# Output stages of a macaron block: low halves of weights on VectorE, sums of activations stored and loaded

## The chip, the cores and the metric

One core of one Trainium2 chip runs the whole program. Time is device time in microseconds of one execution, and the figure for a kernel is the median of its runs. The engines named below are TensorE (PE: matrix products; PEld is its loading of the stationary operand), VectorE (DVE), ScalarE (ACT), GpSimd (POOL) and SyncE (SP, which issues nearly all DMAs here). Each has a queue of its own that is worked off in order.

## The reference

A decoder block on 1024 tokens of width 1024, all float32. The two SwiGLU layers are what this change is about.

```python
def swiglu(x, w_in, w_out):
    gate, up = jnp.split(x @ w_in, 2, axis=-1)      # w_in: 1024 x 5632
    return (jax.nn.silu(gate) * up) @ w_out         # w_out: 2816 x 1024

x = layer_norm(ALPHA * x + 0.5 * swiglu(x, ffn1_w_in, ffn1_w_out), ln1_g, ln1_b)
x = layer_norm(ALPHA * x + token_mixer(x, ...), ln2_g, ln2_b)
x = layer_norm(ALPHA * x + 0.5 * swiglu(x, ffn2_w_in, ffn2_w_out), ln3_g, ln3_b)
e = (p @ ple_w_in) * jax.nn.sigmoid(x @ ple_w_gate)
x = layer_norm(ALPHA * x + e, ln4_g, ln4_b)
```

## The kernel before

Every large float32 product is made of three passes over operands in a rounded format: `split` (lines 176 to 179) casts an operand to its high half on ScalarE and subtracts that from it, on VectorE unless another engine is given, to get the low half; high times high, high times low and low times high are summed in PSUM. Products of 2 x 2 blocks of matrices use Winograd's form of Strassen's scheme: seven block products instead of eight, with sums and differences of blocks on both sides.

**Input stage of a layer** (`ffn`, from line 473; `Pair`, from line 29). The 22 column blocks f of w_in are worked off in the order 0, 10, 1, 11, ..., 9, 19, 20, 21. For each, the weights come as four 256 KB tiles Ws, GpSimd combines them, and seven products of 12 matmuls run (L201). The result silu(gate)*up of 128 features by 1024 tokens lies in two halves g1 and g2 (tiles a) of 512 tokens. `store` writes them to DRAM tensors h, arranged by chunk c of the output stage. The blocks f and f + 10 are the two feature halves of one Strassen block: after f + 10, GpSimd makes from the kept halves of f (`kept`) and the new g2 the sum s2 = kept[1] + g2 - kept[0] in two instructions (lines 529 and 530), and s2 is stored in the place of kept[1]. Tags with few buffers set what may run ahead: T has 6, H and O have 4 each, Ws has 7 and A8 has 14.

**Output stage** (`out_chunk`, from line 576). There are 5 chunks c; chunk c covers the blocks 2c, 2c+1 and their partners. For each chunk `combine` (lines 560 to 574) loads four 128x512 tiles of w_out for each of two blocks j, makes the four combinations t1, t2, t3, t4 on GpSimd (L565, L567, L570, L572; t1, t2 and t4 one after the other in the same tile t), and `put` splits all seven into the tiles w11, wt1, ... (tag A8, so two chunks' worth exist). The low halves of these 14 are made on VectorE in chunk 0 and on GpSimd in chunks 1 to 4 (`gps if c else vec`, line 586). Then for each of the two halves sp of the tokens, ha and hb are loaded (512 KB each, line 594) and hold a11, s2, a12, a22; VectorE makes s1 = s2 + a11, s4 = a12 - s2 and s3 = a22 - s2 (lines 622, 626, 629, tiles s with tag T); each of seven activations is split to Wh and Wl and multiplied with its w (12 matmuls, L603), and VectorE adds the PSUM results into acc or into the sums u (L610, L620, L633). That is 168 matmuls a chunk. After the chunks the two blocks without a partner run in `out_phase` (L232), with the layer norm behind.

The kernel has two such layers, so two input and two output stages. The order of each engine's instructions is fixed when the program is built, by a list scheduler that goes by program order and by estimated times of instructions, so work of the next chunk is placed between that of the current one.

Of the kernel before, what the change touches and what calls it, by code (L numbers as in the profile page):

```python
# [8 lines left out]
F32 = mybir.dt.float32  # L9
# [3 lines left out]
ALU = mybir.AluOpType  # L13
P = 128
# [6 lines left out]
NPAIR = 10  # L21
# [87 lines left out]
class Block:  # L109
# [363 lines left out]
    def ffn(self, xs, w_in, w_out, acc, after, between, points, begun=(None, None), ahead=None, at=None, early=None):  # L473
        staged, later = begun
        nc = self.nc
        gps, vec = nc.gpsimd, nc.vector

        order = FIRST + list(range(2 * NPAIR, NFF))

        def pair(f):  # L480
            def begin(p):
                nc.scalar.activation(p.a1, p.b1, AF.Silu)
            return Pair(self, xs, lambda kh, up: w_in[f + NFF * up][kh], begin,
                        {(kh, up): t for (n, kh), t in (staged or {}).items() for up in range(2) if n == f + NFF * up})

        def products(p):

            marks = iter(range(points if not p.early else 0))

            def tick(ins):  # L490
                if next(marks, None) is not None:
                    with self.tc.issue_after(ins.ins):
                        next(between, None)

            p.rest(tick)
            nc.scalar.activation(p.a2, p.a2, AF.Silu)
            vec.tensor_tensor(p.a1, p.a1, p.c1, ALU.mult)
            tick(vec.tensor_tensor(p.a2, p.a2, p.c2, ALU.mult))
            return p.a1, p.a2

        pairs = self.in_pairs([lambda f=f: pair(f) for f in order], later)

        scale = 0.5 / ALPHA
        chunks = NPAIR // 2
        hd = {}
        for c in range(chunks):
            for kh in range(2):
                hd[c, kh] = self.dram.tile([2, P, 2, 2, 256], F32, tag=f"h{c}_{kh}", name=f"h{c}_{kh}")
        for f in range(2 * NPAIR, NFF):
            hd[f] = self.dram.tile([P, D], F32, tag=f"h{f}", name=f"h{f}")  # L510
        def store(f, th, g):
            if f < 2 * NPAIR:
                c, j = f % NPAIR // 2, f % 2
                dst = hd[c, f // NPAIR][:, :, th, j].rearrange("s p n -> p s n")
                nc.sync.dma_start(dst, g.rearrange("p (s n) -> p s n", n=256))
            else:
                nc.sync.dma_start(hd[f][:, th * 512:(th + 1) * 512], g)

        kept = None
        for i, (f, p) in enumerate(zip(order, pairs)):  # L520
            g1, g2 = products(p)
            store(f, 0, g1)
            if f < NPAIR:
                kept = g1, g2
            else:
                store(f, 1, g2)
            if NPAIR <= f < 2 * NPAIR:

                gps.tensor_tensor(kept[1], kept[1], g2, ALU.add)
                gps.tensor_tensor(kept[1], kept[1], kept[0], ALU.subtract)  # L530
                store(f - NPAIR, 1, kept[1])
            if i == at:
                for _ in between:
                    pass
                early()

        for _ in between:
            pass
        sums = [self.t("E", [P, 512], name="sum") for _ in range(4)]
        for c in range(chunks):  # L540
            self.out_chunk(c, w_out, hd, acc, sums, scale)

        for s in (0, 1, 2, 3, 4, 5, 6, 7):
            for dh in range(2):
                if s >= 4 or dh:
                    sl = slice(dh * 512, (dh + 1) * 512)
                    gps.tensor_tensor(acc[s][:, sl], acc[s][:, sl], sums[s % 4], ALU.add)
        if ahead is not None:
            ahead()
        hs, ws = [], []  # L550
        for f in range(2 * NPAIR, NFF):
            w = self.t("A8", [P, 2, D], F32R, name="wo")
            self.load_row(w_out[f * P:(f + 1) * P, :], w[:, 0], w[:, 1])
            h = [self.t("O", [P, D], F32R, name="hp") for _ in range(2)]
            self.load_row(hd[f], *h)
            hs.append(h)
            ws.append((w[:, 0], w[:, 1]))
        self.out_phase(hs, ws, acc, scale, self.pm, after=after)
# [17 lines left out]
    def out_chunk(self, c, w_out, hd, acc, sums, scale):  # L576


        nc = self.nc
        gps, vec = nc.gpsimd, nc.vector  # L580
        halves = [slice(0, 512), slice(512, 1024)]
        w = {n: self.t("A8", [P, 2, 2, 512], F32R, name="w" + n)
             for n in ("11", "t1", "21", "t2", "22", "t3", "t4")}
        for j in range(2):
            def put(n, y):
                self.split(y, w[n][:, j, 0], w[n][:, j, 1], gps if c else vec)

            b11, b12, b21, b22 = (self.stage(w_out[f * P:(f + 1) * P, halves[dh]])
                                  for f in (2 * c + j, NPAIR + 2 * c + j) for dh in range(2))
            self.combine(b11, b12, b21, b22, put)  # L590
        for sp in range(2):
            ha, hb = self.t("O", [P, 2, 512], name="ha"), self.t("H", [P, 2, 512], name="hb")
            for t, kh in ((ha, 0), (hb, 1)):
                nc.sync.dma_start(t, hd[c, kh][sp].rearrange("p t j n -> p t (j n)"))
            a11, s2, a12, a22 = ha[:, 0], ha[:, 1], hb[:, 0], hb[:, 1]

            def prod(ps, a, n, start=True):
                hh = self.split_w(a)
                for i in range(2):
                    for j in range(2):  # L600
                        cols = slice(256 * j + P * i, 256 * j + P * i + P)
                        for k, (p, q) in enumerate(((0, 0), (0, 1), (1, 0))):
                            nc.tensor.matmul(ps[i], hh[p][:, cols], w[n][:, j, q],  # L603
                                             start=(start and j == 0 and k == 0), stop=(j == 1 and k == 2),
                                             skip_group_check=not start)

            def add(ps, th, dh):
                for i in range(2):
                    t = acc[4 * th + 2 * sp + i][:, halves[dh]]
                    vec.scalar_tensor_tensor(t, ps[i], scale, t, ALU.mult, ALU.add)  # L610

            two = lambda: [self.pm(), self.pm()]
            u = sums[2 * sp:2 * sp + 2]
            b1 = two()
            prod(b1, a11, "11")
            for i in range(2):
                if c == 0:
                    nc.scalar.mul(u[i], b1[i], scale)
                else:
                    vec.scalar_tensor_tensor(u[i], b1[i], scale, u[i], ALU.mult, ALU.add)  # L620
            s1, s3, s4 = (self.t("T", [P, 512], name="s") for _ in range(3))
            vec.tensor_tensor(s1, s2, a11, ALU.add)
            b3 = two()
            prod(b3, s1, "t1")
            add(b3, 1, 1)
            vec.tensor_tensor(s4, a12, s2, ALU.subtract)
            prod(b1, a12, "21", start=False)
            add(b1, 0, 0)
            vec.tensor_tensor(s3, a22, s2, ALU.subtract)
            b2 = two()  # L630
            prod(b2, s2, "t2")
            for i in range(2):
                vec.scalar_tensor_tensor(u[i], b2[i], scale, u[i], ALU.mult, ALU.add)  # L633
            prod(b3, s4, "22", start=False)
            add(b3, 0, 1)
            b4 = two()
            prod(b4, s3, "t3")
            add(b4, 1, 1)
            prod(b4, a22, "t4", start=False)
            add(b4, 1, 0)  # L640
# [689 lines left out]
```

## Time and profile before

| | us |
|---|---|
| median of 3 runs | 2142.65 (2140.26 to 2145.51) |
| profiled execution | 2143.06 |
| its span, first to last instruction | 2141.3 |

| engine | busy us | share of the span |
|---|---|---|
| TensorE | 2008.5 | 94% |
| VectorE | 1682.1 | 79% |
| GpSimd | 1133.6 | 53% |
| ScalarE | 835.8 | 39% |

The page covers the whole program. The first output stage runs from about 474 to 700 us, the second from about 1754 to 1985 us; the input stages lie right ahead of them. Busy times by stretch say more than shares of the whole, since each stage has its own limit. One matmul of 128x512 is listed with some 0.39 us, but matmuls overlap: what counts is the distance from one start to the next. The same holds in part for VectorE, whose instructions overlap by a little.

### The profile page before, as it was taken

To read this page: it belongs to the slowest core of one execution; us is meant where nothing else is said; L and a number is where in the kernel's file an instruction comes from. 1 tells how busy PE (TensorE), PEld (TensorE's weight loads), DVE (VectorE), ACT (ScalarE), POOL (GpSimd) and SP (SyncE) were. 2 spreads that over 40 slices of the span, in tenths; PEclk is the share of its full clock that TensorE was granted. 3 is DMA by queue.
4 is the path that set the end of the run, shared out by engine and by line. 5 is a ranking of instruction groups with operands and counts; after the bars stand their busy time and mean duration, and the time that the engine had idled before them with its cause. 6 is when DMAs were issued, how large, how long until landed. Compare 5 with 4: busy or idle time off the path is not lost.

```text
span 2141.3 us, 26291 instructions
## 1 busy us (share of the span) xinstructions
PE 2008.5 (94%) x8982; PEld 1626.4 (76%) x8982; DVE 1682.1 (79%) x2514; ACT 835.8 (39%) x1492; POOL 1133.6 (53%) x754
## 2 busy tenths in 40 slices
PE   7998999998989899999998899999999998899988
PEld 5886778776768777888885677788888876678866
DVE  8789767678898976667668979966666688898998
ACT  5333333444342454343545524533333343333420
POOL 4646555458972364343236683564444458972360
PEclk9999999999999999999999999999999999999999
DMA  5323233543321254343472240242222243322111
GB/s 171 113 84 94 83 99 113 184 158 123 113 89 44 104 182 140 102 122 110 138 263 66 91 141 15 71 127 89 79 89 79 79 166 115 111 81 79 40 54 69
DMA packets 127702, 228.78 MB, mean 107 GB/s; under 512 B 14160, under 2 KB 43856, under 8 KB 127568
## 3 DMA queue, kind: packets, MB, share of 16 engines
q1 hardware_dynamic: 127568, 227.10, 33.0%
q8 instruction: 71, 1.16, 0.2%
q14 instruction: 63, 0.52, 0.1%
HBM read 174.12 MB, written 52.92 MB: 106 GB/s over the span
## 4 chain that ended last, share of the span: by engine, by line
PE 57%; DVE 20%; POOL 12%; issue 7%; DMA 3%; ACT 2%; SPq 0%; DVEq 0%; POOLq 0%; ACTq 0%
PE pm L201 42%; PE pm L603 7%; DVE Wl L179 3%; POOL wt L179 3%; PE pm L1251 2%; PE pm L212 2%; POOL w L179 2%; POOL t L567 1%; DVE acc L237 1%; PE pm L232 1%; POOL t L572 1%; DVE ln L251 1%; POOL Ws L570 1%; DVE ln L257 1%; POOL t L565 1%
## 5 line engine op out<-in xcount | busy, mean ns | idle before, releaser
L179 DVE TENSOR_TENSOR Wl<-Ws,Wh 128x512 fp32r<-128x512 f32 (+1 forms) x284 | 238.0, 842 | 138.9 <-ACT Wh L178 134.5
L178 ACT CAST Wh<-s 128x512 fp32r<-128x512 f32 (+1 forms) x264 | 158.8, 601 | 383.3 <-PE pm L201 136.1
L178 ACT CAST Wh<-Ws 128x512 fp32r<-128x512 f32 (+1 forms) x284 | 169.5, 597 | 339.3 <-PE pm L201 294.1
L179 DVE TENSOR_TENSOR Wl<-s,Wh 128x512 fp32r<-128x512 f32 (+1 forms) x264 | 227.2, 861 | 35.3 <-ACT Wh L178 35.1
L87 POOL TENSOR_TENSOR s<-s,Ws 128x512 f32<-128x512 f32 (+1 forms) x68 | 95.0, 1397 | 212.8 <-DVE Wl L179 208.0
L603 PE MATMUL pm<-wt,Wh 128*128 128x512 f32 x640 | 190.7, 395 | 2.9 <-ACT Wh L178 2.0
L105 POOL TENSOR_TENSOR u<-u,p 128x512 f32<-128x512 f32 x68 | 109.3, 1607 | 154.1 <-DVE u L95 126.6
L603 PE MATMUL pm<-w,Wh 128*128 128x512 f32 x480 | 149.4, 403 | 22.1 <-ACT Wh L178 17.7
L82 POOL TENSOR_TENSOR s<-Ws 128x512 f32<-128x512 f32 (+1 forms) x68 | 90.6, 1332 | 138.8 <-DVE Wl L179 97.8
L99 POOL TENSOR_TENSOR s<-Ws,s 128x512 f32<-128x512 f32 (+1 forms) x68 | 102.9, 1514 | 110.3 <-DVE Wl L179 110.3
L603 PEld LDWEIGHTS pm<-wt,Wh 128*128 128x128 f32 x640 | 121.5, 191 | 31.3 <-ACT Wh L178 4.8
L610 DVE SCALAR_TENSOR_TENSOR acc<-pm,acc 128x512 f32<-128x512 f32 x200 | 131.7, 681 | 15.6 <-PE pm L603 14.8
L603 PEld LDWEIGHTS pm<-w,Wh 128*128 128x128 f32 x480 | 91.4, 193 | 45.8 <-ACT Wh L178 21.8
L603 PE MATMUL pm<-wt,Wl 128*128 128x512 f32 x320 | 116.6, 398 | 5.5 <-DVE Wl L179 5.5
L603 PE MATMUL pm<-w,Wl 128*128 128x512 f32 x240 | 91.8, 407 | 15.4 <-DVE Wl L179 15.4
L201 PE MATMUL pm<-x11h,Wh 128*128 128x512 f32 (+1 forms) x264 | 99.6, 385 | 5.3 <-ACT x11h L178 4.8
L201 PE MATMUL pm<-x11h,Wl 128*128 128x512 f32 (+1 forms) x264 | 99.7, 380 | 3.3 <-DVE Wl L179 3.3
L201 PE MATMUL pm<-xt2h,Wl 128*128 128x512 f32 x240 | 95.3, 397 | 6.7 <-DVE Wl L179 6.7
L201 PE MATMUL pm<-x11l,Wh 128*128 128x512 f32 (+1 forms) x264 | 99.5, 380 | 2.0 <-DVE x11l L179 1.4
L201 PE MATMUL pm<-xt1h,Wl 128*128 128x512 f32 x240 | 95.0, 396 | 5.4 <-DVE Wl L179 5.3
L91 POOL TENSOR_TENSOR Ws<-Ws 128x512 f32<-128x512 f32 (+1 forms) x68 | 97.4, 1432 | 4.5
L201 PE MATMUL pm<-x21h,Wl 128*128 128x512 f32 x240 | 94.8, 396 | 5.0 <-DVE Wl L179 5.0
(384 smaller groups left out, 5867.1 us busy)
## 6 DMA issues: line engine op xcount, KB each, us to landing
Ws<-in_ffn_w_in SPq DMA_DIRECT2D x196, 256.0 KB, 2.7
Ws<-in_ffn_w_out SPq DMA_DIRECT2D x88, 256.0 KB, 2.9
h<-a SPq DMA_DIRECT2D x78, 256.0 KB, 2.2
Ws<-in_w_mix SPq DMA_DIRECT2D x74, 256.0 KB, 2.7
ha<-h SPq DMA_DIRECT2D x20, 512.0 KB, 4.0
hb<-h SPq DMA_DIRECT2D x20, 512.0 KB, 4.2
acc<-in_x_tok SPq DMA_DIRECT2D x8, 512.0 KB, 7.9
x<-acc SPq DMA_DIRECT2D x8, 512.0 KB, 2.6
```

What stands on the lines that cost most here:

```text
L82: gps.tensor_tensor(s, a21, a22, ALU.add)
L87: gps.tensor_tensor(s, s, a11, ALU.subtract)
L91: gps.tensor_tensor(a21, a11, a21, ALU.subtract)
L99: gps.tensor_tensor(s, a12, s, ALU.subtract)
L105: gps.tensor_tensor(u3, u3, p5, ALU.add)
L178: self.nc.scalar.copy(hi, src)
L179: (lo_eng or self.nc.vector).tensor_tensor(lo, src, hi.bitcast(F32), ALU.subtract)
L201: self.nc.tensor.matmul(ps[:, tok], w[a][:, sl], x[b](k)[:, tok], start=(start and k == 0 and i == 0), stop=(k == nk - 1 and i == 2), skip ...
L212: self.nc.tensor.matmul(ps[h], w[a][:, sl], x(h)[b](k), start=(k == 0 and i == 0), stop=(k == 3 and i == 2))
L603: nc.tensor.matmul(ps[i], hh[p][:, cols], w[n][:, j, q], start=(start and j == 0 and k == 0), stop=(j == 1 and k == 2), skip_group_check=n ...
L610: vec.scalar_tensor_tensor(t, ps[i], scale, t, ALU.mult, ALU.add)
L1251: nc.tensor.matmul(pg, xx[p](k % 4)[:, cols], wg[dh][k][q][:, col], start=(k == 0 and i == 0), stop=(k == NK - 1 and i == 2))
```

## The change

Three things are changed. `put` in `out_chunk` no longer gives an engine, so the low halves of all w are made on VectorE in every chunk. In the input stage, after block f + 10, s1 = kept[1] + g2 and s2 = s1 - kept[0] are made by GpSimd in tiles of their own (s1 in place of p.c2), and s4 = g1 - s2 and s3 = g2 - s2 by VectorE; s1, s4 and s3 are stored with `store_sum` to a new DRAM tensor for each chunk, 256 KB each, s2 as before. In `out_chunk` s1, s3 and s4 are loaded from there, right behind ha and hb, and the three VectorE instructions that made them are gone.

```diff
--- before.py
+++ after.py
@@ -506,6 +506,7 @@
         for c in range(chunks):
             for kh in range(2):
                 hd[c, kh] = self.dram.tile([2, P, 2, 2, 256], F32, tag=f"h{c}_{kh}", name=f"h{c}_{kh}")
+            hd[c, "s"] = self.dram.tile([3, 2, P, 2, 256], F32, tag=f"h{c}_s", name=f"h{c}_s")
         for f in range(2 * NPAIR, NFF):
             hd[f] = self.dram.tile([P, D], F32, tag=f"h{f}", name=f"h{f}")
         def store(f, th, g):
@@ -516,6 +517,10 @@
             else:
                 nc.sync.dma_start(hd[f][:, th * 512:(th + 1) * 512], g)
 
+        def store_sum(f, n, g):
+            dst = hd[f // 2, "s"][n, :, :, f % 2].rearrange("s p n -> p s n")
+            nc.sync.dma_start(dst, g.rearrange("p (s n) -> p s n", n=256))
+
         kept = None
         for i, (f, p) in enumerate(zip(order, pairs)):
             g1, g2 = products(p)
@@ -526,9 +531,16 @@
                 store(f, 1, g2)
             if NPAIR <= f < 2 * NPAIR:
 
-                gps.tensor_tensor(kept[1], kept[1], g2, ALU.add)
-                gps.tensor_tensor(kept[1], kept[1], kept[0], ALU.subtract)
-                store(f - NPAIR, 1, kept[1])
+                s1, s3, s4 = p.c2, kept[1], self.t("T", [P, 512], name="s4")
+                s2 = self.t("T", [P, 512], name="s2")
+                gps.tensor_tensor(s1, kept[1], g2, ALU.add)
+                store_sum(f - NPAIR, 0, s1)
+                gps.tensor_tensor(s2, s1, kept[0], ALU.subtract)
+                store(f - NPAIR, 1, s2)
+                vec.tensor_tensor(s4, g1, s2, ALU.subtract)
+                store_sum(f - NPAIR, 2, s4)
+                vec.tensor_tensor(s3, g2, s2, ALU.subtract)
+                store_sum(f - NPAIR, 1, s3)
             if i == at:
                 for _ in between:
                     pass
@@ -583,7 +595,7 @@
              for n in ("11", "t1", "21", "t2", "22", "t3", "t4")}
         for j in range(2):
             def put(n, y):
-                self.split(y, w[n][:, j, 0], w[n][:, j, 1], gps if c else vec)
+                self.split(y, w[n][:, j, 0], w[n][:, j, 1])
 
             b11, b12, b21, b22 = (self.stage(w_out[f * P:(f + 1) * P, halves[dh]])
                                   for f in (2 * c + j, NPAIR + 2 * c + j) for dh in range(2))
@@ -593,6 +605,9 @@
             for t, kh in ((ha, 0), (hb, 1)):
                 nc.sync.dma_start(t, hd[c, kh][sp].rearrange("p t j n -> p t (j n)"))
             a11, s2, a12, a22 = ha[:, 0], ha[:, 1], hb[:, 0], hb[:, 1]
+            s1, s3, s4 = (self.t("T", [P, 512], name="s") for _ in range(3))
+            for n, t in enumerate((s1, s3, s4)):
+                nc.sync.dma_start(t.rearrange("p (j n) -> p j n", n=256), hd[c, "s"][n, sp])
 
             def prod(ps, a, n, start=True):
                 hh = self.split_w(a)
@@ -618,15 +633,11 @@
                     nc.scalar.mul(u[i], b1[i], scale)
                 else:
                     vec.scalar_tensor_tensor(u[i], b1[i], scale, u[i], ALU.mult, ALU.add)
-            s1, s3, s4 = (self.t("T", [P, 512], name="s") for _ in range(3))
-            vec.tensor_tensor(s1, s2, a11, ALU.add)
             b3 = two()
             prod(b3, s1, "t1")
             add(b3, 1, 1)
-            vec.tensor_tensor(s4, a12, s2, ALU.subtract)
             prod(b1, a12, "21", start=False)
             add(b1, 0, 0)
-            vec.tensor_tensor(s3, a22, s2, ALU.subtract)
             b2 = two()
             prod(b2, s2, "t2")
             for i in range(2):
```

## Rows read from the trace of the kernel before

**Rows 1.** The page: span, and busy time by engine (us, share, instructions)

```profile
span 2141.3 us, 26291 instructions
PE 2008.5 (94%) x8982; PEld 1626.4 (76%) x8982; DVE 1682.1 (79%) x2514; ACT 835.8 (39%) x1492; POOL 1133.6 (53%) x754
```

**Rows 2.** Busy time by stretches of the output stages (first columns: stretch, length)

```profile
core 0: us, PE busy (x) PEld busy (x) DVE busy (x) ACT busy (x) POOL busy (x), PEclk, DMA share, GB/s
474.00:500.00 26.00, 18.14 (x67) 13.01 (x68) 26.00 (x32) 11.41 (x22) 16.08 (x10) 0.93 0.69 236
500.00:640.00 140.00, 124.47 (x530) 99.23 (x529) 123.79 (x154) 56.52 (x100) 130.56 (x82) 0.99 0.31 102
640.00:700.00 60.00, 60.00 (x266) 49.68 (x265) 52.06 (x83) 14.78 (x26) 15.19 (x11) 1.00 0.15 45
1754.00:1780.00 26.00, 18.85 (x61) 14.07 (x62) 26.00 (x32) 9.56 (x18) 14.22 (x9) 0.80 0.68 241
1780.00:1920.00 140.00, 126.58 (x531) 100.44 (x530) 122.16 (x152) 55.46 (x100) 129.49 (x82) 0.98 0.31 102
```

**Rows 3.** The same for the input stages

```profile
1480.00:1700.00 220.00, 220.00 (x972) 182.19 (x971) 141.21 (x173) 75.15 (x128) 97.13 (x70) 1.00 0.28 84
...
20.00:474.00 454.00, 434.75 (x1959) 351.13 (x1958) 347.15 (x566) 171.16 (x309) 256.32 (x162) 0.98 0.34 108
...
1320.00:1754.00 434.00, 425.72 (x1896) 349.89 (x1894) 303.27 (x387) 169.37 (x298) 211.94 (x147) 1.00 0.30 88
```

**Rows 4.** Who waited for whom, 500 to 640 us (total us, times, longest)

```profile
ACT wt L178 <- POOL t L567: 23.0, 7, 6.9
ACT wt L178 <- POOL t L572: 21.0, 7, 4.9
...
PE pm L603 <- ACT Wh L178: 8.1, 4, 3.2
```

**Rows 5.** The same of the low halves (line 179) alone: VectorE, then GpSimd

```profile
500.00:640.00 140.00, 45.52 (x45) 84.04 (x53) 0.99 0.31 102
...
1480.00:1700.00 220.00, 64.19 (x81) 0.00 (x0) 1.00 0.28 84
640.00:660.00 20.00, 9.30 (x14) 0.00 (x0) 1.00 0.25 80
474.00:500.00 26.00, 10.95 (x14) 5.68 (x4) 0.93 0.69 236
```

**Rows 6.** VectorE's groups by line, 500 to 640 us (busy us, mean ns, idle)

```profile
L610 DVE SCALAR_TENSOR_TENSOR acc<-pm,acc 128x512 f32<-128x512 f32 x64 | 41.7, 678 | 0.8 <-PE pm L603 0.6
...
L629 DVE TENSOR_TENSOR s<-hb,ha 128x512 f32<-128x512 f32 x7 | 10.7, 1527 | 0.2
L622 DVE TENSOR_TENSOR s<-ha 128x512 f32<-128x512 f32 x7 | 10.2, 1455 | 0.2
...
L626 DVE TENSOR_TENSOR s<-hb,ha 128x512 f32<-128x512 f32 x6 | 7.6, 1261 | 0.0
```

**Rows 7.** Timeline of VectorE, 494 to 497 us (start, length)

```profile
495.35 1.28 DVE L610 SCALAR_TENSOR_TENSOR acc<-pm,acc 128x512 f32<-128x512 f32 x2
496.55 0.68 DVE L179 TENSOR_TENSOR wt<-t,wt 128x512 fp32r<-128x512 f32 x1
```

**Rows 8.** Who waited for whom, 20 to 474 us

```profile
PE pm L201 <- DVE Wl L179: 15.3, 12, 3.2
```

**Rows 9.** VectorE's groups by line, 474 to 500 us

```profile
L626 DVE TENSOR_TENSOR s<-hb,ha 128x512 f32<-128x512 f32 x3 | 4.7, 1575 | 0.0
...
L622 DVE TENSOR_TENSOR s<-ha 128x512 f32<-128x512 f32 x3 | 3.1, 1034 | 0.0
...
L629 DVE TENSOR_TENSOR s<-hb,ha 128x512 f32<-128x512 f32 x2 | 2.4, 1218 | 0.0
```

**Rows 10.** DMA of 474 to 500 us in 40 equal slices

```profile
GB/s 343 400 388 391 406 372 350 340 384 432 397 400 255 158 303 76 32 372 221 309 265 82 170 365 186 214 167 38 0 0 25 202 340 243 132 249 19 113 268 22
```

**Rows 11.** What SP's queue waited for, 1320 to 1754 us

```profile
SPq L515 <- DVE a L498: 57.8, 10, 6.9
```

## The prediction

> **What bounds the kernel now.** I read the page first: TensorE is busy 94% of a span of 2141.3 us, so what can be won is only what it stands still or runs slowly, and the question is where [rows 1]. The table by stretches answers that. In the input stage from 1480 to 1700 us TensorE never stops: 972 matmuls in 220.00 us, 0.2263 us each [rows 3]. With this pitch each stretch of the output stages has a price. From 500 to 640 us there are 530 matmuls, 119.9 us of work in 140: 20.1 us are lost. From 474 to 500 there are 67, 15.2 us of work in 26: 10.8 us lost. The second output stage repeats it: 19.8 us lost from 1780 to 1920 and 12.2 us from 1754 to 1780 [rows 2]. From 640 to 700, when all weights are made, nothing is lost (266 matmuls are 60.2 us) [rows 2]. The output stages thus lose 62.9 us together, clock dips included (granted clock 0.93 and 0.80 in the two opening stretches [rows 2]), and this is the most that the change can give back there.
>
> Who holds TensorE up? In the two long stretches GpSimd is busy 93% (130.56 of 140 us) [rows 2], and ScalarE, whose queue is in order, stands 44 us in front of casts of the weight combinations t that GpSimd has yet to make (L567, L572); the cast of the next activations Wh lies behind these, and TensorE then waits for Wh [rows 4]. In the opening stretches GpSimd is not it: VectorE is busy 26.00 of 26 us [rows 2], and these are the stretches where chunk 0's low halves are already made on VectorE. So the profile shows two different limits, and the change works on one and leans on the other.
>
> **Part 1, low halves of the weights from GpSimd to VectorE (chunks 1 to 4).** 14 a chunk, 56 an output stage, 112 in all. From 500 to 640 GpSimd makes 53 of them in 84.04 of its 130.56 us [rows 2, 5]; 46.5 us for 29 combinations stay, so its share falls from 93% to about 33%. VectorE gets 53 instructions. Back to back one takes 0.60 us (two adds and the next start lie at 495.35 and 496.55) [rows 7]; with GpSimd working beside it an instruction with two SBUF inputs takes longer by x. The rows give x against GpSimd's share: at no GpSimd work 0 (14 in 9.30 us), at 97.13/220 = 44% 0.12 (64.19/81 = 0.79, against 0.68 for one that meets nothing), at 93% 0.33 (45.52/45 = 1.01) [rows 2, 3, 5]. For 33% the nearest row is that of 44%; in proportion x = 0.09, and I take 0.10, with 0 and 0.33 as ends.
>
> **Part 2, the sums s1, s3, s4 are loaded instead of made.** VectorE loses 20 instructions from 500 to 640, 10.7 + 10.2 + 7.6 = 28.5 us [rows 6], and in 474 to 500 eight in three groups, 4.7 + 3.1 + 2.4 = 10.2 us [rows 9].
>
> **VectorE's account for 500 to 640.** Kept: 64 adds into acc and the 25 into the sums u (154 less 64, 45 and 20 [rows 2, 5, 6]), of about 0.68 us each though GpSimd is busy beside them (one of their inputs is in PSUM) [rows 6], 89 x 0.60 = 53.4 us. Two-input ones: 45 low halves of activations and 53 of weights, 98 x (0.60 + x). With x = 0.10 the sum is 53.4 + 68.6 = 122.0 us; with 0 it is 112.2, with 0.33 it is 144.5. The account of before, with 0.08 us of overlap taken off each, is 53.4 + (45.5 - 3.6) + (28.5 - 1.6) = 122.2 us, near the measured 123.79 [rows 2, 5, 6]. So VectorE has no less to do than today: GpSimd is relieved, and VectorE then sets the pace at 122.0 against TensorE's 119.9. An in-order engine that feeds another doesn't stay full; I allow 5% (VectorE is full in the opening stretches and 88% in this one [rows 2]): 122.0/0.95 = 128 us instead of 140, a gain of 12 us a stage.
>
> **The opening stretch.** VectorE loses 10.2 us and gets the four low halves that GpSimd makes there today (5.68 us on GpSimd [rows 5]; 4 x 0.70 = 2.8 us on VectorE), so it is relieved by 7 us of 26; I count 5 of the 10.8 lost us as won. Against it stand the loads: six of 256 KB for chunk 0, beside transfers that already move 340 to 432 GB/s in the first 8 us [rows 10]. At 390 GB/s they are 4.0 us if all of it stands ahead of what TensorE waits for, and 0 if the queue puts them early; I take 1.5. Net 3.5 us a stage. In the closing stretch TensorE is full already, so six sums fewer there give nothing.
>
> **Part 3, the input stages.** Each of the 10 paired blocks gets two VectorE subtractions, 40 in all, 0.60 to 1.5 us each (the sums of today take up to that [rows 6]): 24 to 60 us of VectorE time, 0 of it on the path where TensorE has cover. GpSimd keeps two instructions a block. VectorE stands idle 107 of 454 us and 131 of 434 [rows 3], and that hides them. TensorE waits 15.3 us for VectorE's low halves in the first input stage, 4.4% of VectorE's 347 busy us [rows 8, 3]; the same share of 20 x 0.95 = 19 us is 0.8 us. Two risks are added: s4 and s3 wait for GpSimd's s2, and behind them on VectorE stand the low halves Wl that TensorE needs; and SP gets 60 stores. Its queue is in order, it already stands up to 6.9 us in front of a store [rows 11], and weight loads lie behind. If each of the 20 blocks paid one GpSimd instruction of about 1.6 us (46.5/29 [rows 2, 5]) it would be 32 us; if none, 0. I take 4 us for both stages, near the low end, because TensorE has no idle time at all in 1480 to 1700 although such stores are there now [rows 3, 11]. In the output stage SP also issues 60 loads more; each sum's buffer comes free only when the stage two halves of a chunk back has been split, so the next chunk's weight loads stand behind it. They have a whole half chunk, 84 x 0.2263 = 19 us, so I put this at nothing; without that cover it is part of the 5% above.
>
> **The sum.** 2 x (12 + 3.5) = 31 us won, 4 us paid: 2143.06 - 31 + 4 = **2116 us**. That is against the profiled execution's own 2143.06 us (its span of 2141.3 and 1.8 around it); the median shown is 2142.65, 0.4 us lower, which I don't carry.
>
> **Rivals.** (B) TensorE alone bounds: x is near 0, as where GpSimd is idle [rows 5], the 20 us of the long stretch come back whole and 8 of the opening one. For it: 0.60 us pitch leaves VectorE 112.2 of 119.9 us. Against it: combinations still take a third of GpSimd's time. 2 x 28 = 56 won: **2088 us**. (C) The wait moves but stays: each low half that starts beside a GpSimd instruction waits out half of it, x = 0.33 x 1.6/2 = 0.26, so 53.4 + 98 x 0.86 = 137.7 us of VectorE, 138 full and 145 at 95%, about today's 140: nothing won in the long stretch; 2 x 3.5 won and 4 paid: **2140 us**. For it: GpSimd's combinations now wait for VectorE's low half of the same tile t before they overwrite it, so the two engines take turns. Against it: at 44% the row gives 0.12. Beside it stands the Trainium skill, "SBUF — State Buffer", section "Who interferes with whom": a VectorE instruction with two SBUF inputs contends with a GpSimd instruction that reads SBUF, and the one that comes second is blocked for the whole of the other. Also "Perfetto Trace Analysis", section "Optimizing Scalar/DVE Operations", which says that moving work between these two might not help. The contention is in the trace (1.01 against 0.68 us), but the row at 44% has less than half of what blocking whole instructions would make, 0.44 x 0.8 = 0.35; by that rule the time is C's, by the row it is the forecast's. (D) Slower: VectorE itself becomes the bound by more than is won. The place is the low halves of chunks 1 to 4. It decides from x = (140 - 53.4)/98 - 0.60 = 0.28; with x = 0.33 as today, 144.5/0.95 = 152, 12 us lost a stage, and 3.5 won: 2143 + 17 + 4 = **2164 us**. For it: the opening stretches are just that, VectorE full with low halves and TensorE losing 42% [rows 2]. Against it: half of what fills VectorE there is sums that go away.
>
> **How the numbers follow.** Likeliest case 50%, its own range 2102 to 2128; B 13%; C 21%, 2128 to 2150; D 16%, above 2150. The kernel is measured to about 0.3%, 6.4 us, so faster means below 2136.2 and slower above 2149.1: faster 50 + 13 + about 9 of C = 72%, same 12%, slower 16%. The range 2090 to 2150 leaves out D and the lower part of B.
>
> **What would show it.** Right: from 500 to 640 GpSimd near a third, VectorE above 90%, hardly any wait of ScalarE for t L567 or L572, TensorE's remaining waits for Wl on VectorE; low halves of weights at about 0.75 us; opening stretch with fewer lost us but VectorE still full; input stage 1480 to 1700 still near 220 us. Wrong: low halves at 1 us or more (C, D), TensorE waiting for loads of the sums or of weights behind stores, or VectorE with slack and TensorE full (B).

## The result and the profile after

The changed kernel takes 2112.6 us (median of 4 runs, 2109.2 to 2114.4), the kernel before 2141.45 in the runs beside it: 28.9 us less by the medians, and a ratio of 0.9854, 95% interval 0.9841 to 0.9868, which is 31 us (28 to 34). The forecast was 2116. The profiled execution took 2109.2 us, its span 34.1 us less than that of before.

Where the 34.1 us lie can be read from the starts of the matmuls in the two traces. From the first output product (L603 before, L618 after) to the last matmul of `out_phase` (L232) the first output stage falls from 244.1 to 225.2 us and the second from 245.8 to 227.3: 18.9 and 18.5 us won. The last matmul of the first input stage starts 3.2 us later (476.6 against 473.4), and the first output product follows after 3.2 us instead of 0.5: 2.7 us more. The second input stage is as long as before (436.5 against 436.7 us; the expectation printed with Part 3 below has both 0.2 us shorter, since it stops one group of matmuls early). The mixer between and the tail are 1.8 and 0.8 us shorter, though nothing was changed in them, which says how far single us can be trusted.

Busy time by stretches of the kernel after, laid as those of [rows 2] with the stretches moved along with the stage:

```profile
480.00:506.00 26.00, 24.35 (x106) 19.59 (x107) 24.16 (x34) 14.96 (x28) 13.75 (x9) 1.00 0.86 314
506.00:640.00 134.00, 127.75 (x548) 101.35 (x548) 131.99 (x197) 57.11 (x99) 37.63 (x27) 1.00 0.49 152
640.00:700.00 60.00, 60.00 (x267) 49.63 (x266) 51.01 (x98) 13.51 (x20) 17.96 (x12) 1.00 0.10 31
1740.00:1766.00 26.00, 25.42 (x102) 19.60 (x102) 26.00 (x36) 14.60 (x28) 11.94 (x8) 0.93 0.87 307
1766.00:1900.00 134.00, 127.34 (x546) 100.89 (x545) 131.10 (x194) 58.28 (x101) 39.22 (x27) 1.00 0.46 147
```

With the pitch of 0.2263 us the long stretches now hold 548 and 546 matmuls, 124.0 and 123.6 us of work in 134: 10.0 and 10.4 us lost, against 20.1 and 19.8. The opening stretches lose 26 - 106 x 0.2263 = 2.0 and 2.9 us, against 10.8 and 12.2; the granted clock in them rose from 0.93 and 0.80 to 1.00 and 0.93. GpSimd has fallen from 93% to 28%, and VectorE is now the full one: 131.99 of 134 us, 98%. The waits of the first long stretch say the same (total us, times, longest):

```profile
POOL t L579 <- DVE wt L179: 34.5, 7, 12.7
POOL t L584 <- DVE wt L179: 13.8, 7, 4.8
...
PEld pm L618 <- DVE Wl L179: 8.7, 10, 1.8
ACT wt L178 <- POOL t L579: 8.0, 7, 2.3
ACT wt L178 <- POOL t L584: 6.7, 3, 4.9
...
PE pm L618 <- DVE Wl L179: 4.7, 6, 1.3
...
ACT wt L178 <- POOL t L577: 3.5, 2, 1.8
...
ACT wt L178 <- POOL Ws L582: 0.8, 2, 0.6
```

Three rows of the kernel before, from the view of [rows 4], belong beside them:

```profile
ACT wt L178 <- POOL Ws L570: 9.1, 4, 4.2
...
ACT wt L178 <- POOL t L565: 7.6, 4, 3.7
...
PE pm L603 <- DVE Wl L179: 6.9, 4, 2.7
```

ScalarE stood 44 us in front of t in [rows 4], and 60.7 us in front of all four combinations; that is 14.7 and 19.0 now. Instead GpSimd waits for VectorE, since it may not overwrite t before its low half is made. TensorE's waits for casts Wh on ScalarE (8.1 us before) are gone, and 4.7 us of waits for low halves Wl on VectorE are left. These were there before too: 6.9 us, which [rows 4] does not list. So in the long stretch TensorE stood for VectorE nearly as long as for casts before the change; not all of it is VectorE's own doing, since VectorE itself waited 15.0 us there for casts Wh. The low halves (line 179) alone, in the long stretches and in an input stage, to be read against [rows 5]:

```profile
506.00:640.00 134.00, 79.55 (x103) 0.00 (x0) 1.00 0.49 152
...
1766.00:1900.00 134.00, 79.69 (x102) 0.00 (x0) 1.00 0.46 147
1466.00:1686.00 220.00, 71.08 (x81) 0.00 (x0) 1.00 0.34 105
```

All 103 are on VectorE, 0.77 us each by busy time over count. That must be held against the same measure of low halves that meet nothing, 0.65 us in the kernel without combinations below, and not against 0.68 us, which is the length of one instruction (neighbours overlap): x is 0.12, where the forecast had put 0.10. It is not spread evenly. By mean length of one instruction (the number behind the busy time, in ns), in the first long stretch:

```profile
L179 DVE TENSOR_TENSOR wt<-t,wt 128x512 fp32r<-128x512 f32 x22 | 20.3, 925 | 0.0
L179 DVE TENSOR_TENSOR w<-Ws,w 128x512 fp32r<-128x512 f32 x20 | 16.6, 841 | 0.0
L179 DVE TENSOR_TENSOR Wl<-s,Wh 128x512 fp32r<-128x512 f32 x20 | 14.0, 702 | 0.0
```

Most low halves take 0.68 us; those that run while GpSimd works take up to 1.78 us, 1.1 more. In the input stage the mean rose from 0.79 to 0.88 us (71.08/81) although GpSimd's share did not change there, 44% before and 45% after:

```profile
1466.00:1686.00 220.00, 220.00 (x972) 182.16 (x971) 159.62 (x185) 74.79 (x129) 98.72 (x69) 1.00 0.34 105
```

So GpSimd's share alone does not say how long a low half takes; what else meets it there was not tried. TensorE loses nothing in this stretch, as before.

### The profile page after: what moved, and what is told of

Read it like the earlier page. It is cut to its first block, busy times and chain, and to the rows that moved or that the text cites. A ratio compares the mean times of both kernels' runs of the same rounds, so it can differ in the third digit from the quotient of the medians.

```text
span 2107.2 us, 26598 instructions
## 1 busy us (share of the span) xinstructions
PE 2000.9 (95%) x8982; PEld 1621.0 (77%) x8982; DVE 1719.4 (82%) x2606; ACT 838.2 (40%) x1492; POOL 945.8 (45%) x642
## 4 chain that ended last, share of the span: by engine, by line
PE 56%; DVE 22%; issue 5%; POOL 3%; DMA 3%; ACT 2%; DVEq 0%; SPq 0%; POOLq 0%; ACTq 0%
PE pm L201 38%; PE pm L618 10%; DVE Wl L179 4%; DVE wt L179 2%; PE pm L1262 2%; PE pm L212 2%; DVE acc L625 1%; DVE w L179 1%; DVE acc L237 1%; PE pm L232 1%; DVE ln L251 1%; POOL x L1139 1%; DMA Ws<-in_ffn_w_out 1%; DVE ln L257 1%; PE pt L1267 1%
## 5 line engine op out<-in xcount | busy, mean ns | idle before, releaser
L618 PE MATMUL pm<-wt,Wh 128*128 128x512 f32 x640 | 188.5, 393 | 3.4 <-DVE acc L625 3.1
L618 PE MATMUL pm<-w,Wh 128*128 128x512 f32 x480 | 141.0, 392 | 6.7 <-ACT Wh L178 6.7
L618 PEld LDWEIGHTS pm<-wt,Wh 128*128 128x128 f32 x640 | 119.5, 188 | 32.0 <-DVE acc L625 4.2
L618 PE MATMUL pm<-wt,Wl 128*128 128x512 f32 x320 | 113.1, 392 | 4.4 <-DVE Wl L179 4.2
L618 PEld LDWEIGHTS pm<-w,Wh 128*128 128x128 f32 x480 | 90.1, 189 | 26.7 <-ACT Wh L178 7.9
L201 PE MATMUL pm<-x21h,Wh 128*128 128x512 f32 x240 | 95.2, 397 | 2.2 <-ACT Wh L178 2.2
```

Of the source, the lines that this page charges most:

```text
L201: self.nc.tensor.matmul(ps[:, tok], w[a][:, sl], x[b](k)[:, tok], start=(start and k == 0 and i == 0), stop=(k == nk - 1 and i == 2), skip ...
L618: nc.tensor.matmul(ps[i], hh[p][:, cols], w[n][:, j, q], start=(start and j == 0 and k == 0), stop=(j == 1 and k == 2), skip_group_check=n ...
```

## The experiments

In all of them "lost" is a stretch less its matmuls at 0.2263 us, as in the prediction.

**Part 1 alone.** In the kernel before, one line:

```diff
-                self.split(y, w[n][:, j, 0], w[n][:, j, 1], gps if c else vec)
+                self.split(y, w[n][:, j, 0], w[n][:, j, 1])
```

> Part 1 alone: the kernel before with the low halves of all weights on VectorE; the sums s1, s3, s4 are still made on VectorE in the output stage. My theory (VectorE's account sets the pace of the long stretch once GpSimd is relieved): the account of the changed kernel is 132 us of 134 in its long stretch, and 20 sums come back to it, 20 x (0.60 + 0.10) = 14 us, about 146 us against the 140 of the kernel before; the opening stretch keeps its sums, so its loss stays near 11 us or grows by the four low halves. Together 0 to 8 us lost a stage: 2140 to 2158 us. Rival (what held TensorE was only ScalarE standing in front of casts that GpSimd was late with; the sums don't matter): the whole gain of the long stretches is there without the loads, about 2 x 10 us, 2118 to 2125 us.

Measured: 2140.5 us, ratio 0.9987 (0.9977 to 0.9996), 2.4 us less by the medians and 2.8 (0.9 to 4.9) by the ratio. Its opening stretch and the two long ones:

```profile
476.00:502.00 26.00, 19.30 (x71) 14.02 (x72) 26.00 (x36) 10.77 (x20) 10.13 (x6) 0.93 0.68 238
502.00:640.00 138.00, 127.80 (x523) 97.49 (x522) 136.75 (x204) 56.96 (x100) 46.32 (x29) 0.98 0.32 103
...
1780.00:1920.00 140.00, 126.90 (x523) 95.95 (x522) 139.96 (x205) 57.04 (x100) 43.43 (x29) 0.99 0.31 102
```

VectorE is full (136.75 of 138, 139.96 of 140), GpSimd down to a third, and TensorE loses 19.6 and 21.6 us as it did before, with 9.9 in the opening stretch. The rival, that relieving GpSimd brings the gain by itself, falls: the limit only moved from one engine to the other. In the waits TensorE stands 10.0 us for VectorE there (6.8 for adds into acc, 3.2 for Wl) and 0.3 for ScalarE's casts. This is the half of the change that the title puts first.

**Parts 2 and 3 alone.** The changed kernel with `gps if c else vec` put back.

> Parts 2 and 3 alone: the changed kernel with the low halves of the weights of chunks 1 to 4 back on GpSimd; the sums are stored and loaded. My theory (two limits, each removed by its own part): the opening stretches, where VectorE was full, give back about 9 us each; in the long stretches GpSimd is over 90% busy as before and ScalarE still stands about 40 us in front of t, though VectorE is only about two thirds busy, so 15 to 20 us stay lost there: about 2141 - 18 + 4 = 2127 us, 2120 to 2134. Rival (VectorE's sums were the limit in both stretches, GpSimd's lateness only a symptom): the long stretches come back too, 2085 to 2105 us.

Measured: 2120.2 us, ratio 0.9906 (0.9884 to 0.9929), at the low edge of what my theory gave. First the opening and the long stretch, then the waits of the long one:

```profile
481.00:507.00 26.00, 23.68 (x101) 18.16 (x100) 22.58 (x30) 13.86 (x26) 23.03 (x14) 1.00 0.88 310
507.00:640.00 133.00, 125.25 (x526) 100.95 (x525) 97.59 (x135) 54.93 (x99) 114.41 (x78) 0.96 0.45 143
```

```profile
ACT wt L178 <- POOL t L579: 12.6, 6, 3.7
ACT wt L178 <- POOL t L584: 11.6, 6, 2.9
ACT wt L178 <- POOL Ws L582: 8.3, 3, 3.7
ACT wt L178 <- POOL t L577: 6.2, 3, 4.4
```

The opening stretch has nearly its whole gain without Part 1 (3.1 us lost, 2.0 with both). In the long stretch VectorE is down to 73%, yet 14.0 us stay lost (13.1 in the second stage): GpSimd is at 86% and ScalarE stands 39 us in front of the four combinations that it has yet to make (60.7 before). Yet the sums alone won 6.1 us of the first long stretch and 6.7 of the second, so they are more than room on VectorE. They also relieved GpSimd, one of whose low halves takes 72.57/50 = 1.45 us here and took 84.04/53 = 1.59 in [rows 5]:

```profile
507.00:640.00 133.00, 46.26 (x49) 72.57 (x50) 0.96 0.45 143
```

So each part alone leaves one engine in the way, and together they are worth more than one by one: by the medians 2 us for Part 1, 23 for the sums, 29 for both, by the ratios 3, 20 and 31. Of the whole, the low halves add 8 us (medians, 2120.2 to 2112.6) to 11 us (ratios) to what the sums bring.

**Part 3 alone.** The sums are made and stored in the input stages, and `out_chunk` is that of the kernel before, so that the stored sums are read by nobody.

```diff
-            s1, s3, s4 = (self.t("T", [P, 512], name="s") for _ in range(3))
-            for n, t in enumerate((s1, s3, s4)):
-                nc.sync.dma_start(t.rearrange("p (j n) -> p j n", n=256), hd[c, "s"][n, sp])
...
+            vec.tensor_tensor(s1, s2, a11, ALU.add)
...
+            vec.tensor_tensor(s4, a12, s2, ALU.subtract)
...
+            vec.tensor_tensor(s3, a22, s2, ALU.subtract)
...
-                self.split(y, w[n][:, j, 0], w[n][:, j, 1])
+                self.split(y, w[n][:, j, 0], w[n][:, j, 1], gps if c else vec)
```

> Part 3 alone: the kernel before with the sums made and stored in the input stages, but the output stages as they were (the stored sums are read by nobody). It measures the term that the prediction put at 4 us for both input stages. In the changed kernel the first input stage ended 3.2 us later and the second took 436.3 us against 436.5. If the term is as there: 2 to 6 us more than the kernel before, 2144 to 2150 us; if the 3 us came from the output stage's weights placed into the end of the input stage, no change: 2140 to 2145 us.

Measured: 2146.5 us, ratio 1.0014 (1.0006 to 1.0023), 3.0 us on 2142.3, with 1.3 to 4.9 as its interval (4.2 us by the medians). The last matmul of the first input stage starts at 478.8 us instead of 473.4; the second takes 436.8 us, 436.7 before. (With Part 1 alone, which leaves the input stage as it was, the first ended at 475.4, so some 2 us of such a difference need not come from the sums.) The waits of TensorE there, against 15.3 us in [rows 8] and 16.8 with Part 1 alone:

```profile
PE pm L201 <- DVE Wl L179: 19.3, 14, 3.5
```

**The order of the loads.** The loads of s1, s3, s4 are traced behind the first product of each half chunk:

```diff
-            s1, s3, s4 = (self.t("T", [P, 512], name="s") for _ in range(3))
-            for n, t in enumerate((s1, s3, s4)):
-                nc.sync.dma_start(t.rearrange("p (j n) -> p j n", n=256), hd[c, "s"][n, sp])
...
             prod(b1, a11, "11")
+            s1, s3, s4 = (self.t("T", [P, 512], name="s") for _ in range(3))
+            for k, t in enumerate((s1, s3, s4)):
+                nc.sync.dma_start(t.rearrange("p (j n) -> p j n", n=256), hd[c, "s"][k, sp])
```

> The changed kernel with the three loads of the sums traced behind the first product of each half chunk, so that ha and hb go first. In the changed kernel four loads of sums stand ahead of ha at 468.3 us, ha is issued at 473.2 instead of 468.8 us and the first product of the first output stage starts 2.8 us after the queue of the input stage is done, 0.7 us in the kernel before. If the order of the loads makes that gap, it falls to about 1 us in the first stage and the time by 1 to 3 us, 2109 to 2112; if the gap comes from the transfers themselves or from the last input block, nothing changes: 2112 to 2115.

Measured: 2110.9 us, within the spread of the changed kernel, and the gap is the same (476.7 to 479.8 us). The run doesn't decide the question, since the scheduler put the loads where they had been; SP's timeline of this kernel:

```profile
468.37 1.85 SPq L630 DMA_DIRECT2D s<-h_s  x4
471.71 0.33 SPq L183 DMA_DIRECT2D Ws<-in_ffn_w_out  x1
472.87 0.32 SPq L630 DMA_DIRECT2D s<-h_s  x1
473.24 1.47 SPq L606 DMA_DIRECT2D ha<-h  x2
```

**No combinations.** Is VectorE's load what still loses 10 us a stage? The changed kernel without GpSimd's four combinations of the weights in the output stages; the blocks themselves are split in their place, so this part of the computation is left out.

```diff
-            self.combine(b11, b12, b21, b22, put)
+            for n, b in (("11", b11), ("t1", b12), ("t2", b22), ("21", b21), ("t3", b12), ("t4", b21), ("22", b22)):
+                put(n, b)
```

> The changed kernel without GpSimd's four combinations of the weights in the output stages (the blocks themselves are split in their place, so that part of the computation is left out); everything on VectorE, ScalarE and TensorE stays. My theory (VectorE is the bound at 132 of 134 us, and 0.09 us of each of its two-input instructions is GpSimd beside it, plus low halves that wait in turn with GpSimd for one tile): low halves fall to 0.68 us, the account of the long stretch to about 122 us, TensorE bounds, and most of the 10 us still lost in each long stretch come back: 2092 to 2102 us. Rival (VectorE is full only because the order of the queues makes it catch up; TensorE's loss comes from PSUM banks or ScalarE): 2107 to 2113 us.

Measured: 2095.0 us, ratio 0.9781 (0.9767 to 0.9796). The long stretches, and the low halves in the first:

```profile
507.00:640.00 133.00, 133.00 (x588) 110.13 (x587) 119.63 (x194) 54.30 (x95) 0.00 (x0) 1.00 0.45 139
...
1760.00:1900.00 140.00, 140.00 (x618) 115.67 (x617) 128.58 (x211) 62.70 (x110) 0.00 (x0) 1.00 0.47 147
```

```profile
507.00:640.00 133.00, 62.45 (x96) 0.00 (x0) 1.00 0.45 139
```

588 matmuls are 133.1 us: TensorE loses nothing. VectorE is at 90% and a low half takes 0.65 us. So neither PSUM banks nor ScalarE's own work is in the way. What this run takes away is all that hangs on the combinations: GpSimd's reading beside VectorE, the turns of the two engines on the tile t, ScalarE's waits for combinations, and one of the seven Ws buffers that t takes.

**Combinations into a tile that nobody reads.** As the last one, but GpSimd makes its four subtractions a block nevertheless.

```diff
+            t1 = self.t("Ws", [P, 512], name="t1")
+            for n, b, x, y in (("11", b11, None, None), ("t1", b12, b12, b11), ("t2", b22, b22, t1), ("21", b21, None, None),
+                               ("t3", b12, b22, b12), ("t4", b21, b21, t1), ("22", b22, None, None)):
+                if x is not None:
+                    gps.tensor_tensor(t1, x, y, ALU.subtract)
+                put(n, b)
```

> As e4 (the blocks of the weights are split in place of their combinations, so that part of the computation is left out), but GpSimd runs its four subtractions a block nevertheless, into a tile that nobody reads. It tells apart the two things that e4 took away at once: GpSimd's reading beside VectorE, and the turns that GpSimd and VectorE take on one tile t. If the contention is the price: the low halves are back at 0.75 to 0.80 us, VectorE over 95% busy, and 6 to 10 us a long stretch are lost: 2105 to 2113 us. If the turns are the price: low halves may be longer than 0.68 us but TensorE stays full as in e4: 2093 to 2099 us.

Measured: 2120.6 us, ratio 0.9894 (0.9879 to 0.9908), above both expectations. The opening and the long stretch, and the low halves in the latter:

```profile
481.00:507.00 26.00, 20.03 (x78) 15.76 (x79) 24.11 (x31) 12.83 (x24) 9.38 (x7) 0.87 0.85 312
507.00:640.00 133.00, 128.05 (x551) 103.46 (x550) 127.15 (x191) 56.00 (x98) 45.59 (x27) 0.99 0.47 148
```

```profile
507.00:640.00 133.00, 76.39 (x100) 0.00 (x0) 0.99 0.47 148
```

In the long stretches most of the loss is back with the contention: 0.76 us a low half, VectorE at 96%, 8.3 and 9.1 us lost, though no low half depends on what GpSimd makes. The Ws buffer is taken again as well; ScalarE waits 2.0 us for loads of weights in the first long stretch, so a small part may be that. What lies above the expectation is in the opening stretches, which lose 8.3 and 9.3 us. In the first stands one wait of TensorE, part of it ahead of the stretch, for a cast that follows the last block's activation on ScalarE:

```profile
PE pm L623 <- ACT Wh L178: 7.9, 1, 7.9
```

That is another order of the queues, not the cause in question; the second opening stretch was not followed up.

**Some low halves back on GpSimd.** In the changed kernel, 2, 4 and 6 of 14 a chunk:

```diff
-                self.split(y, w[n][:, j, 0], w[n][:, j, 1])
+                self.split(y, w[n][:, j, 0], w[n][:, j, 1], gps if c and n == "22" else vec)
...
+                self.split(y, w[n][:, j, 0], w[n][:, j, 1], gps if c and n in ("22", "11") else vec)
...
+                self.split(y, w[n][:, j, 0], w[n][:, j, 1], gps if c and n in ("22", "21", "11") else vec)
```

> The changed kernel, but GpSimd makes 2 of the 14 low halves of a chunk (those of w22) in chunks 1 to 4. My theory (VectorE full at 132 of 134 us, GpSimd with 96 us free): 7 low halves less in the long stretch are 5.4 us, of which the higher contention (GpSimd's share from 28% to 35%) takes about 2 back; 3 us less lost a stage: 2105 to 2109 us. If VectorE is not what sets the pace, no change: 2111 to 2114.

> As e5 with 4 of 14 (w11 and w22) on GpSimd. By the account 14 low halves less on VectorE, 10.8 us, 3 to 4 taken back by contention; VectorE then has 125 us against 124 of TensorE: 2101 to 2106 us. Against it: w11 is the first that each chunk needs.

> As e5 with 6 of 14 (w11, w21, w22: the blocks that are no combination, so no low half on GpSimd is part of a chain through t). By the account VectorE has about 121 us against 124 of TensorE, GpSimd about half its time: no more is won than by 4, 2099 to 2106 us; if lateness on GpSimd holds TensorE again as in e2 (14 of 14 there, 2120 us), 2106 to 2113.

Measured: 2115.3, 2113.6 and 2112.0 us (ratios 0.9869, 0.9864 and 0.9851, each with about 0.0015 to either side; 0.9854 is the changed kernel's). Nothing is won by any, where 4 to 14 us had been expected. The long stretch with 6 of 14, all engines and then the low halves:

```profile
507.00:640.00 133.00, 127.27 (x546) 103.60 (x545) 124.78 (x175) 56.62 (x99) 69.92 (x47) 0.97 0.49 153
```

```profile
507.00:640.00 133.00, 71.46 (x81) 30.25 (x20) 0.97 0.49 153
```

VectorE has fewer instructions (175 against 197 in a stretch 1 us longer), but a low half takes 71.46/81 = 0.88 us instead of 0.77, with GpSimd at 53%. TensorE loses 9.4 us as before although VectorE is at 94% and not full. Of TensorE's waits there, 5.5 us of 5.7 are for Wl on VectorE and none is for GpSimd. So my account by VectorE's amount of work is not the whole: I read it that what counts is also how long the single low half takes that TensorE is waiting for; no run changes that length alone.

**Everything on VectorE.** The consequence of the last two: the combinations in the output stages are made on VectorE as well, by an engine that `combine` is given.

```diff
-    def combine(self, b11, b12, b21, b22, put):
+    def combine(self, b11, b12, b21, b22, put, eng=None):
...
-        gps = self.nc.gpsimd
+        eng = eng or self.nc.gpsimd
...
-            self.combine(b11, b12, b21, b22, put)
+            self.combine(b11, b12, b21, b22, put, vec)
```

> The changed kernel with GpSimd's four combinations of the weights made on VectorE too, in the output stages; GpSimd has nothing to do there then. If contention is the price as e4 and e7 say, every two-input instruction falls to 0.60 us back to back: kept adds 53.4 us, low halves 98 x 0.60 = 58.8, combinations 29 x 0.60 = 17.4, together 129.6 us against 132 measured in the changed kernel, so VectorE is as full as before and the loss of a long stretch stays at 8 to 11 us: 2107 to 2115 us. If it is the amount of VectorE's work that counts and contention little, 29 instructions more cost up to 17 us a stage: 2130 to 2147 us.

Measured: 2101.2 us (2100.8 to 2103.2), ratio 0.9802 (0.9788 to 0.9815): better than the forecast by my theory, and 11 us faster than the changed kernel. The long stretches and three of VectorE's groups in the first (from 507 us):

```profile
505.00:640.00 135.00, 132.53 (x575) 106.09 (x574) 134.91 (x225) 58.66 (x100) 0.00 (x0) 1.00 0.46 147
...
1759.00:1890.00 131.00, 128.09 (x556) 103.21 (x556) 131.00 (x219) 59.49 (x103) 0.00 (x0) 1.00 0.47 146
```

```profile
L625 DVE SCALAR_TENSOR_TENSOR acc<-pm,acc 128x512 f32<-128x512 f32 x67 | 44.7, 690 | 0.0
L179 DVE TENSOR_TENSOR wt<-t,wt 128x512 fp32r<-128x512 f32 x21 | 14.5, 691 | 0.1
...
L582 DVE TENSOR_TENSOR Ws<-Ws 128x512 f32<-128x512 f32 x7 | 4.8, 691 | 0.0
```

VectorE is busy 134.91 of 135 us with 225 instructions, all of 0.69 us, and TensorE loses 4.9 and 5.2 us, half of the changed kernel's. More work on the fuller engine made the kernel faster: 225 instructions start every 0.60 us (134.91/225), and each low half is done after 0.69 us. ScalarE still stands 18 us in front of combinations in the first long stretch, as it did in the changed kernel (19.0), so that wait is not what was removed. That the chain through t no longer crosses to GpSimd may help as well; this was not tried by itself.

## Why the prediction was right, step by step

**The limits were read rightly, but not sharply.** GpSimd in the long stretches and VectorE in the opening ones [rows 2]: each part alone leaves the other limit, as the two halves of the change run by themselves show. What the reading left out is that in the long stretch TensorE waited for VectorE as well (6.9 us against 8.1 for casts).

**VectorE's account held, in part by luck.** x was put at 0.10 and measured 0.12; the long stretch was to have VectorE above 90% and has it at 98%; GpSimd was to fall near a third and fell to 28%. The gain of a long stretch was put at 12 us and is 10.1 and 9.4. Two errors cancel in it. For as many matmuls as in the forecast, 530, VectorE worked 127.7 us instead of 122.0 (131.99 x 530/548), with 190 instructions instead of 187 and a larger x; but it left 2% idle instead of 5%, so the stretch came to 129.6 us instead of 128. The slack was not what TensorE loses: with 6 low halves of 14 back on GpSimd, VectorE has 6% idle and the loss is the same. The way to x was weaker than its result. The forecast's rows take 0.68 us, one instruction's length, from busy time over count; 0.79 - 0.68 is 0.11 and not 0.12, and against the 0.66 of its own row without GpSimd it is 0.13. And x was taken in proportion to GpSimd's share, while the input stage shows 0.79 us at 44% before and 0.88 at 45% after.

**The signs.** TensorE's waits for Wl, the full VectorE and the full input stage came as named. ScalarE's wait in front of t did not become "hardly any": 14.7 of 44 us stayed. Low halves of weights were to take about 0.75 us; in the largest groups they take 0.84 and 0.93, and those of the sums 0.70.

**The opening stretch was mis-sized.** 5 us were counted of a relief of 7, and 8.8 and 9.3 came, with the sums alone (7.7 us in the first). VectorE was full there, and more came back than the 7 us that were taken off it, with the clock's rise in it; to count two thirds had no row behind it. The loads were charged 1.5 us a stage; 2.7 us show as the later first product in the first stage and 0.2 in the second. The rows of the kernel after show two things that hold this first product up. One is the order of a queue:

```profile
477.87 0.68 DVE L102 TENSOR_TENSOR a<-pm,u 128x512 f32<-128x512 f32 x1
...
478.58 0.63 ACT L496 ACTIVATE a<-a 128x512 f32<-128x512 f32 x1 [1.14 <-DVE a L102]
479.16 0.62 ACT L178 CAST Wh<-ha 128x512 fp32r<-128x512 f32 x1
...
479.83 1.19 PE L618 MATMUL pm<-w,Wh 128*128 128x512 f32 x4 [2.82 <-ACT Wh L178]
```

The cast of the first activation stands on ScalarE behind the last block's activation, which waits for VectorE's L102, which starts at 477.87 us among chunk 0's low halves; in the kernel before that cast came first, at 473.20 against 475.97 us. The other is the load of ha. The rows show its issue before, its issue after, its time from issue to landing after (the shortest was 4.0 us before), and the cast in the kernel with everything on VectorE:

```profile
468.83 1.92 SPq L594 DMA_DIRECT2D ha<-h  x3
...
473.19 1.77 SPq L606 DMA_DIRECT2D ha<-h  x2
...
DMA to landing us min/median/max: 5.9/5.9/6.8
...
478.30 0.62 ACT L178 CAST Wh<-ha 128x512 fp32r<-128x512 f32 x1 [0.42 <-DMA ha<-h]
```

Issued 4.4 us later than before (the input stage ends 3.2 us later), behind the loads of the sums, ha lands at about 479.1 us, just as the cast starts: without the activation ahead of it the cast could not have come earlier. In the kernel with everything on VectorE the activation is done in time, the cast waits for ha itself, and the gap is still 2.3 us, against 3.2 in the changed kernel and 0.5 before. So ha's late landing accounts for most of the gap. How much of that is the loads of the sums alone is not shown, since the edit that was to move them left their places as they were.

**The input stages** were put at 4 us and cost 3.0 (1.3 to 4.9) when run alone, nothing of it in the second. The reason given, cover by idle VectorE time, holds where TensorE never stopped; the first input stage, where TensorE already waited for VectorE [rows 8], paid: these waits rose from 15.3 to 19.3 us.

**The sum.** 2 x 17 was forecast for the two stretches of an output stage, 18.9 + 18.5 came; against it 3 for the loads, where 2.7 + 0.2 came, and 4 for the input stages, where 3.2 - 0.2 came; 2.6 us fell in stages that the change doesn't touch. That the total is so near is partly luck: the opening stretches gave 18.1 us instead of 10 and the long ones 19.5 instead of 24, and this cancels in part.

**The rivals.** (B) would have needed x near 0; it is what the kernel without combinations shows, 2095.0 us, and it needs GpSimd out of the way. (Its own sum gives 2087, and leaves out the 4 us of the input stages.) (C) needed x = 0.26 at a third of GpSimd's time; measured is 0.12 at 28%. Its mechanism is there (GpSimd waits 34.5 and 13.8 us for low halves of t in the two largest rows above), but GpSimd has that time. The Trainium skill's rule in "SBUF — State Buffer", "Who interferes with whom", is that the shared ports of the two engines are an exclusive lock. The traces agree in kind: an instruction with two SBUF inputs is longer beside GpSimd (up to 1.78 us) and back at 0.68 to 0.69 us without it, and the adds that read PSUM stay at 0.68 to 0.69. By size they do not: blocking for half of an instruction of 1.4 us at 28% would be 0.20 us by my estimate, and 0.12 is measured. The Trainium skill's "Perfetto Trace Analysis", "Optimizing Scalar/DVE Operations", says that moving work between these two might not help. The trace agrees for the low halves moved alone (2 us); with the sums gone the same move brought 8 us, and moving the combinations as well 11 more. (D) fell: its point, x = 0.28, is far off.

**What was not seen.** The prediction treated the gain of the long stretch as that of Part 1, with the sums as room on VectorE. The runs split it otherwise: 23 of 29 us come with the sums alone, and in the long stretches 6.1 and 6.7 us where Part 1 alone wins nothing (0.5 us less lost in the first, 1.8 more in the second). And it priced GpSimd's remaining combinations only as x in VectorE's account, not as something to be moved too.

## What to carry to other kernels

When an engine is full and its neighbour is moved onto or off it, run both halves of such a change by themselves: here the low halves by themselves were worth 2 us and the sums 23, and they needed each other for 29. A busy share near 100% says who sets the pace but not what is lost: VectorE at 98% lost 10 us of TensorE's time with instructions that GpSimd made longer, and 5 us at 100% with undisturbed ones. Before sharing work between VectorE and GpSimd, ask whether one of them alone, uncontended, does it all in the time there is.

## What the runs showed of the hardware that I had not expected

Work given back to GpSimd bought nothing. With more of GpSimd's time VectorE's two-input instructions were longer (busy time of line 179 over its count: at 0, 28, 39, 46 and 53% of GpSimd's time one took 0.66, 0.77, 0.86, 0.85 and 0.88 us), and with 2, 4 or 6 instructions fewer of 14 the time stayed at 2112 to 2115 us. The share is not the whole of it: at 45% in an input stage one took 0.88 us, and 0.76 at 34% in the kernel whose combinations nobody reads. And 28 more instructions in such a stretch on a VectorE that was 98% busy went with a program 11 us faster, all of its instructions there at 0.69 us.
